# Two-unit lag for attention's transposes and values, later convolution products, and conditioning vectors from fp32r parts

## The chip, the cores and the metric

The kernel runs on one core of one Trainium2 chip. The metric is the device time of one execution in microseconds (us), as a median over runs. A difference of about 0.2% (6 us) is the least that a measurement of this kernel tells from no change.

The engines: PE (TensorE, matrix products), DVE (VectorE), ACT (ScalarE), POOL (GpSimd) and SP (which issues DMAs). Each engine takes its instructions in the order in which the program writes them; semaphores hold one engine back for another.

## The reference

Two layers of an encoder trunk are applied to a prompt of 512 tokens and to a sample of 256 tokens, width 1024. Cut to what matters here:

```python
for l in range(DEPTH):                                    # DEPTH = 2
    mod = (silu(c) @ ada_w[l] + ada_b[l]).reshape(B, 9, D)     # conditioning vectors
    h = x * (1 + mod[:, 1]) + mod[:, 0]
    x = layer_norm(ALPHA * x + 0.5 * (1 + mod[:, 2]) * swiglu_1(h))
    h = x * (1 + mod[:, 4]) + mod[:, 3]
    q, k, v, hz = split(h @ w_in[l])
    o_attn = window_attention(rope(q), rope(k), v, sink[l])    # |i - j| <= 128, softmax with a sink
    x0, x1, hv = split(short_conv(hz))
    filt = hyena_filters(L, ...)       # FFN with three sines, times a decay window
    o_hy = bidir_long_conv(hv * x1, filt) * x0                 # spectra: U * K, then inverse
    o = concat(rms_norm(o_attn), rms_norm(o_hy)) @ w_out[l]
    x = layer_norm(ALPHA * x + (1 + mod[:, 5]) * o)
    ...                                                        # second SwiGLU, layer norm
```

The diff touches three places of it: the first two conditioning vectors of layer 0, the long convolution, and the attention.

## The kernel before

**Numbers.** A product of two fp32 matrices is made of fp32r parts: ACT copies a tile to fp32r (the high part, `acopy`), DVE subtracts it from the original (the low part, `tt`), and PE runs three fp32r products, high by high, high by low, low by high. A plain fp32 product needs no parts, and shows as two records per product in the trace.

**Order.** The schedule is written by hand: every engine runs its instructions in program order. Tiles live in slots (`slot_s` 10, `slot_w` 6, `slot_r` 7, `slot_t` 6, `tiny` 12, and the 8 PSUM banks), and an allocation takes the free slot whose last use is oldest. All instructions come from one recording helper, so the profile shows them all at line 70; they are told apart by their tiles.

**The prologue** (from line 940). The filter FFN has three layers of `mlp` (two fp32 products on PE) and `sine` (seven DVE instructions and one ACT sine). Between them stand the calls of `ada_mm`: for i in 0 to 15, two fp32 products on 512 columns of `cc` (the silu of c) with a 512 KB tile of `ada_w`. The order is: sine 0, `ada_mm` 0 and 1, sine 1, `ada_mm` 2 to 4, sine 2, the decay rows of the filter, `ada_mm` 5 to 7, then six rounds of `tokens(t)` with `ada_mm(8 + t)`, a flush, `ada_mm` 14 and 15, and the spectra of the filters. `tokens(t)` is two fp32 products of 64 rows on PE, two multiplications by the window on DVE, the next window on ACT, and the split of the round before (two ACT copies, one subtraction on DVE, one on POOL). In rounds 0 and 4 DVE also adds a bias, in rounds 4 and 5 a sum and a difference.

**The mixer** (`run` in `mixer`, once per layer). Projection units 4 to 11 (48 products each) feed the convolution. `Hyena.products(a)` is DVE work: 16 tensor_tensor instructions on 512 columns for a = 0 and 1, 8 for a = 2, with ACT copies between; `inverse(a)` is 24 products on PE, `gate(a)` one DVE multiplication out of a bank. There are two Hyena halves, `hy0` and `hy1`, each with a = 0, 1, 2. `unit(i)` also calls `w_ahead(2)`, which splits the next weights (ACT copy, DVE subtraction). Then come three groups g of projections in three token pairs tp for keys and values and for the two halves of the queries: PE products, an ACT copy, rope on DVE, a split, and one step later the transposes of the result on PE (`transposed`). After each of these nine steps `side(i)` puts in other work.

**Attention** (`attention`, `Attention`). There are 12 units u of four heads each; units 4 to 7 of the key blocks in the middle have 384 keys (u = 6 to 9), the others 256. For one unit: `scores` (8 products on PE, then on DVE a masked copy with its maximum for each head, and small terms), `exps` (4 exponentials on ACT), `norms` (DVE sum and reciprocal, then the scaling of four heads), `turned` (8 or 12 transposes on PE and an ACT copy to high parts), `turned_lo` (DVE low parts), `values` (6 or 9 products on PE, ACT copy to `oT`). Round u of the loop runs `scores(u)`, `turned(u-1)`, `exps(u)`, `turned_lo(u-1)`, `filler`, `norms(u)`, `values(u-1)`. A `filler` is 12 products of the output projection on 512 and 256 columns; every second one ends in two DVE additions. `block_squares` (ACT square, two DVE additions) and the RMS steps stand between. DVE's own order in a round is thus: the maxima of `scores(u)`, `turned_lo`, `block_squares`, RMS steps, `norms(u)`, additions, and then the maxima of `scores(u+1)`.

Of the kernel before, what the change touches and what calls it, by code (L numbers as in the profile page):

```python
# [17 lines left out]
P = 128  # L18
D = 1024
# [141 lines left out]
def _program(mem, nc, x_in, c_col, c_row, w_units, ada_nat, ada_t, ada_b, ln_p, conv_p, sink_in, grp_in,  # L161
# [26 lines left out]
    def f32(ap):  # L188
        return ap.bitcast(F32)
# [764 lines left out]
    sp.dma_start(cc, c_col)  # L954
    act.activation(out=cc, in_=cc, func=AF.Silu)
    pa = [bank() for _ in range(4)]
    ada_raw = [slot_q([D]) for _ in range(4)]
# [8 lines left out]
    def ada_mm(i):  # L966
        raw = ada_raw[i]
        k, half = i // 2, i % 2
        for q in range(2):
            mm(pa[2 * half + q][:2, :512], cc[:, k, :], raw[:, q * 512:(q + 1) * 512], k == 0, k == ND - 1)  # L970
        if i + 4 < 16:
            ada_raw.append(slot_q([D]))
            sp.dma_start(ada_raw[i + 4], ada_nat[i + 4])
# [161 lines left out]
    def mods_part(i):  # L1135
        if i < 4:
            ams.append(slot_t([512]))
            acopy(ams[i][:2], pa[i][:2, :512])
        i -= 1
        am = ams[i] if i >= 0 else None  # L1140
        for j in range(4 if i >= 0 else 0):
            n = 4 * i + j
            pe.transpose(bt[:, 2 * n:2 * n + 2], am[:2, j * P:(j + 1) * P], idf[:2, :2])

# [4 lines left out]
    def skip():  # L1149
# [6 lines left out]
    gp.dma_start(ab, ada_b[:, 0, :2 * ND])  # L1156
    tt(mods[0][:, 0:2].rearrange("p m d s -> p (m d) s"), bt[:, :32].rearrange("p (n s) -> p n s", s=2),
       ab.unsqueeze(2).to_broadcast([P, 2 * ND, 2]), ALU.add)
    G, B = modul(0, 0, None)
# [27 lines left out]
    def mixer(l, x_prev, hh, hl):  # L1187
# [183 lines left out]
        def run(end):  # L1371
# [12 lines left out]
            u_transposes(1)  # L1384
            hy0.products(2)
            proj.unit(9)
            hy0.gate(0)
            hy0.inverse(1, dinv)
            hy1 = Hyena(1, u_spectrum(1, dfw))
            hy0.gate(1)  # L1390
            hy0.inverse(2, dinv)
            hy1.products(0)
            proj.unit(10)
            hy0.gate(2)
            hy1.products(1)
            proj.unit(11)
            hy1.inverse(0, dinv)
            hy1.products(2)
            hy1.gate(0)

# [4 lines left out]
            def side(i):  # L1405
                if i == 0:
                    hy1.inverse(1, dinv)
                    hy1.gate(1)
                elif i == 1:
                    hy1.inverse(2, dinv)  # L1410
                    hy1.gate(2)
                    rms[0].squares()
                elif i == 2:
                    rms[1].squares()
# [98 lines left out]
        class Attention:  # L1513
# [48 lines left out]
            def norms(self, u):  # L1562
                k0, k1 = self.keys(u)
                n = (k1 - k0) * P
                pv, sm = self.p[u], self.tinies.pop(u)
                es, den, rd = (sm[:, 4 * i:4 * i + 4] for i in range(3, 6))
                tt(den, den, es, ALU.add)
                vec.reciprocal(rd, den)
                for h in range(4):
                    if h < 2:  # L1570
                        ts(pv[:, h, :n], pv[:, h, :n], rd[:, h:h + 1], None)
                    else:
                        act.activation(out=pv[:, h, :n], in_=pv[:, h, :n], func=AF.Copy, scale=rd[:, h:h + 1])

# [30 lines left out]
        def attention(at, rms, on_hy, last_q, end):  # L1605
# [26 lines left out]
            fill = [(d, ks) for d in range(6) for ks in ((0, 1), (2, 3))]  # L1632
            share = (0, 0, 1, 1, 1, 1, 1, 1, 1, 1, 1, 2)
            fbank = {}
# [16 lines left out]
            rms_at = [Rms(oT, 0, s) for s in range(2)]  # L1651
            for u in range(1, 13):
                if 1 < u < 12:
                    at.scores(u)
                if u > 1:
                    at.turned(u - 1)
                    if u < 12:
                        at.exps(u)
                else:
                    filler()  # L1660
                    last_q()
                if u > 1:
                    at.turned_lo(u - 1)
                if done:
                    block_squares(done.pop())
                if u == 1:
                    rms[0].apply(on_hy, (2, 3))
                elif u == 2:
                    rms[1].apply(on_hy, (2, 3))
                    reload()  # L1670
                elif u == 6:
                    rms_at[1].Q = Q[0][:, SEQ[1]]
                    rms_at[1].stats()
                elif u == 7:
                    rms_at[1].bcast()
                    on_at.append(slot_s([2, 2, T], F32R))
                elif u == 8:
                    rms_at[1].apply(on_at, (0, 1))
                elif u == 11:
                    on_at.append(slot_s([2, 2, T], F32R))  # L1680
                    rms_at[1].apply(on_at, (2, 3))
                adds = [filler() for _ in range(share[u - 1])]
                if u < 12:
                    at.norms(u)
                for add in adds:
                    add()
                at.values(u - 1, oT)
                if at.units[u - 1][1]:
                    done.append(at.units[u - 1][0])
            block_squares(done.pop())  # L1690
# [235 lines left out]
```

## Time and profile before

| what | value |
|---|---|
| time, median of 3 runs | 2938.31 us (2937.6 to 2939.61) |
| time of the profiled execution | 2938.19 us |
| its span, first to last instruction | 2936.2 us |
| PE busy | 2837.5 us (97%) |
| DVE busy | 2139.2 us (73%) |
| ACT busy | 1367.5 us (47%) |
| POOL busy | 331.8 us (11%) |
| mean granted TensorE clock | 0.987 of full speed |

The profiled execution lasted 2.0 us more than its span and lies 0.1 us from the median of the runs, so a change of the span can be added to the median. The stages: prologue 0 to about 126 us, mixers about 690 to 1010 and 2090 to 2410 us, SwiGLU parts elsewhere. A view of waits lists who waited for whom, with the total, the number of times and the longest; a timeline lists instructions of one engine in order of time, equal neighbours merged (x12 means twelve), with the idle time before and its releaser in brackets. A merged line's time runs from the first start to the last end.

### The profile page before, as it was taken

The numbers are of one execution on the slowest core, as the hardware profiler recorded it, in microseconds if no ns is written. First come the engines' busy times: TensorE is split into PE (matmuls) and PEld (weight loads), VectorE is DVE, ScalarE is ACT, GpSimd is POOL, SyncE is SP. The second block draws the span as 40 slices with busy tenths as digits, with TensorE's granted clock in tenths as the row PEclk, the third lists the DMA queues.
The fourth block names the chain that finished last, engine by engine and source line by source line (L and its number), as shares of the span: only waits on it lengthen the run. The fifth ranks groups of instructions, "written<-read, shape, count | busy, mean of one in ns | idle before, by whom it ended". The sixth has DMA issues, their size and how long they took to land. (4 is left out here: it accounts for less than half of the span.)

```text
span 2936.2 us, 42164 instructions
## 1 busy us (share of the span) xinstructions
PE 2837.5 (97%) x16468; PEld 2594.4 (88%) x16468; DVE 2139.2 (73%) x3821; ACT 1367.5 (47%) x2355; POOL 331.8 (11%) x394
## 2 busy tenths in 40 slices
PE   9999999999998999999999999999999899999998
PEld 3789999988887889999988999998888788999997
DVE  5788778878967887777588777557896787444558
ACT  3544444444366544444445444444436644444444
POOL 2400000031000300000030000002100030000000
PEclk9999999999999999999999999999999999999999
DMA  5546665542121135664333665344212112455332
GB/s 202 194 171 173 188 176 164 147 151 103 57 73 51 65 127 161 194 194 116 107 122 122 179 176 157 107 107 145 102 63 73 51 57 89 85 115 115 97 108 83
DMA packets 102607, 364.65 MB, mean 124 GB/s; under 512 B 13750, under 2 KB 17031, under 8 KB 99208
## 3 DMA queue, kind: packets, MB, share of 16 engines
q1 hardware_dynamic: 74968, 259.88, 24.5%
q0 software_dynamic: 27440, 102.08, 16.2%
q8 instruction: 129, 2.11, 0.3%
q14 instruction: 70, 0.57, 0.1%
HBM read 284.33 MB, written 80.74 MB: 124 GB/s over the span
## 5 line engine op out<-in xcount | busy, mean ns | idle before, releaser
L70 PE MATMUL bank<-slot_s,slot_w 128*128 128x384 f32 (+2 forms) x13176 | 2322.1, 336 | 44.0 <-DVE slot_s L70 26.7
L70 PEld LDWEIGHTS bank<-slot_s,slot_w 128*128 128x128 f32 x13176 | 2130.5, 190 | 212.2 <-DVE slot_s L70 23.0
L70 DVE TENSOR_TENSOR slot_w<-slot_w,slot_w 128x1024 fp32r<-128x1024 f32 (+2 forms) x444 | 370.0, 864 | 4.1 <-ACT slot_w L70 1.6
L70 DVE CUSTOM_DVE_ANT_0 slot_t<-slot_r,slot_r 128x1024 bf16<-128x1024 f32 x256 | 311.4, 1223 | 77.4 <-DMA x_spill<-slot_t 45.0
L70 ACT ACTIVATE slot_w<-slot_w 128x1024 fp32r<-128x1024 f32 (+1 forms) x298 | 249.7, 838 | 119.2 <-DVE slot_w L70 118.9
L70 DVE TENSOR_TENSOR slot_w<-slot_r,slot_w 128x1024 fp32r<-128x1024 f32 (+1 forms) x194 | 222.0, 1153 | 113.4 <-ACT slot_w L70 111.9
L70 ACT ACTIVATE slot_t<-bank,tiny 128x512 f32<-128x512 f32 (+1 forms) x256 | 147.5, 580 | 307.9 <-PE bank L70 302.1
L70 POOL DMA_DIRECT2D x_spill<-slot_t x128 | 110.4, 862 | 1409.2 <-ACT slot_t L70 1409.2
L70 ACT ACTIVATE slot_w<-slot_r 128x1024 fp32r<-128x1024 f32 (+1 forms) x194 | 189.0, 992 | 155.9 <-DVE slot_r L70 98.1
L70 ACT ACTIVATE slot_t<-slot_t 128x384 f32<-128x384 f32 (+2 forms) x161 | 84.1, 526 | 334.2 <-DVE slot_t L70 334.0
L70 DVE TENSOR_TENSOR slot_t<-bank,slot_t 128x384 f32<-128x384 f32 x228 | 125.5, 555 | 144.2 <-PE bank L70 73.5
L70 DVE TENSOR_TENSOR slot_s<-slot_t,slot_s 128x768 fp32r<-128x768 f32 (+2 forms) x190 | 153.1, 810 | 52.6 <-ACT slot_s L70 48.4
L70 ACT ACTIVATE slot_s<-slot_t 128x768 fp32r<-128x768 f32 (+2 forms) x160 | 113.8, 717 | 159.9 <-DVE slot_t L70 155.5
L70 ACT ACTIVATE slot_t<-bank 128x384 f32<-128x384 f32 (+3 forms) x282 | 139.6, 495 | 101.6 <-PE bank L70 99.1
L70 PE MATMUL bank<-slot_s,slot_r 128*128 128x384 f32 x912 | 172.0, 337 | 0.0
L70 PEld LDWEIGHTS bank<-slot_s,slot_r 128*128 128x128 f32 x912 | 160.6, 188 | 0.0
L70 DVE TENSOR_TENSOR slot_r<-slot_w,slot_r 128x512 fp32r<-128x512 f32 x76 | 52.0, 684 | 106.4 <-ACT slot_r L70 106.4
L70 ACT ACTIVATE slot_t<-slot_s 128x256 f32<-128x256 f32 (+1 forms) x132 | 65.9, 510 | 108.0 <-DVE slot_s L70 104.1
L70 PE MATMUL bank<-slot_w,slot_s 128*128 128x256 f32 x864 | 107.9, 284 | 3.1 <-DVE slot_w L70 1.8
L70 PEld LDWEIGHTS bank<-slot_w,slot_s 128*128 128x128 f32 x864 | 104.7, 191 | 3.9 <-DVE slot_w L70 2.1
L70 DVE SCALAR_TENSOR_TENSOR slot_t<-bank,slot_t 128x384 f32<-128x384 f32 x76 | 42.3, 556 | 83.4 <-PE bank L70 82.2
L70 DVE SCALAR_TENSOR_TENSOR slot_s<-bank,tiny,slot_s 128x256 f32<-128x256 f32 (+1 forms) x160 | 87.0, 564 | 15.1 <-PE bank L70 14.9
(137 smaller groups left out, 2132.2 us busy)
## 6 DMA issues: line engine op xcount, KB each, us to landing
slot_r<-w_units SPq DMA_DIRECT2D x170, 512.0 KB, 4.8
slot_w<-w_units SPq DMA_DIRECT2D x146, 512.0 KB, 4.1
slot_r<-ada_t SPq DMA_DIRECT2D x128, 512.0 KB, 5.8
x_spill<-slot_t POOLq DMA_DIRECT2D x128, 384.0 KB, 5.3
slot_s<-x_spill POOLq DMA_DIRECT2D x12, 1536.0 KB, 8.2
x_spill<-slot_s POOLq DMA_DIRECT2D x10, 1024.0 KB, 4.6
slot_r<-ada_nat SPq DMA_DIRECT2D x16, 512.0 KB, 5.9
g_main<-slot_s POOLq DMA_DIRECT2D x4, 1536.0 KB, 10.0
```

The lines of the kernel that those rows point to most:

```text
L70: return getattr(real, name)(*args, **kwargs)
```

## The change

In the prologue `cc` is split into two parts in a tile of four columns (`cs`), and `ada_mm` splits each 512 KB tile (ACT copy, DVE subtraction) and multiplies both parts: four fp32r products instead of two fp32 products. The four rows of the result are transposed and added in pairs. In the mixer `hy0.products(2)` moves from behind the transposes of `hy1` to behind `hy0.gate(1)`; `hy1.products(0)` and `hy0.inverse(2)` move by one unit, and the three inverses of `hy1`, with `hy1.products(2)`, move into `side(0)` to `side(2)`. In the attention `turned` and `values` of a unit come two rounds behind its scores instead of one, with a thirteenth round at the end; fillers go one to a round from the second to the twelfth; RMS steps move by one round; in `norms` three heads are scaled on DVE and the fourth on POOL, where two were on DVE and two on ACT.

```diff
+    cs = const("cs", [ND, 4], F32R)
+    acopy(cs[:, :, 0:2], cc)
+    tt(cs[:, :, 2:4], cc, f32(cs[:, :, 0:2]), ALU.subtract)
...
         k, half = i // 2, i % 2
+        w = slot_w([2, D])
+        acopy(w[:, 0], raw)
+        tt(w[:, 1], raw, f32(w[:, 0]), ALU.subtract)
         for q in range(2):
-            mm(pa[2 * half + q][:2, :512], cc[:, k, :], raw[:, q * 512:(q + 1) * 512], k == 0, k == ND - 1)
+            for part in range(2):
+                mm(pa[2 * half + q][:4, :512], cs[:, k, :], w[:, part, q * 512:(q + 1) * 512],
+                   k == 0 and part == 0, k == ND - 1 and part == 1)
...
             u_transposes(1)
-            hy0.products(2)
             proj.unit(9)
             hy0.gate(0)
             hy0.inverse(1, dinv)
             hy1 = Hyena(1, u_spectrum(1, dfw))
             hy0.gate(1)
+            hy0.products(2)
+            proj.unit(10)
+            hy1.products(0)
+            proj.unit(11)
             hy0.inverse(2, dinv)
-            hy1.products(0)
-            proj.unit(10)
             hy0.gate(2)
             hy1.products(1)
-            proj.unit(11)
-            hy1.inverse(0, dinv)
-            hy1.products(2)
-            hy1.gate(0)
...
                 if i == 0:
+                    hy1.inverse(0, dinv)
+                    hy1.gate(0)
+                elif i == 1:
                     hy1.inverse(1, dinv)
+                    hy1.products(2)
                     hy1.gate(1)
-                elif i == 1:
+                    rms[0].squares()
+                elif i == 2:
                     hy1.inverse(2, dinv)
                     hy1.gate(2)
-                    rms[0].squares()
-                elif i == 2:
                     rms[1].squares()
...
                 for h in range(4):
-                    if h < 2:
-                        ts(pv[:, h, :n], pv[:, h, :n], rd[:, h:h + 1], None)
-                    else:
-                        act.activation(out=pv[:, h, :n], in_=pv[:, h, :n], func=AF.Copy, scale=rd[:, h:h + 1])
+                    ts(pv[:, h, :n], pv[:, h, :n], rd[:, h:h + 1], None, eng=gp if h == 3 else vec)
...
-            share = (0, 0, 1, 1, 1, 1, 1, 1, 1, 1, 1, 2)
+            share = (0,) + (1,) * 12
...
-            for u in range(1, 13):
+            o_hy.ahead = 1
+            for u in range(1, 14):
                 if 1 < u < 12:
                     at.scores(u)
-                if u > 1:
-                    at.turned(u - 1)
-                    if u < 12:
-                        at.exps(u)
-                else:
+                if u > 2:
+                    at.turned(u - 2)
+                if 1 < u < 12:
+                    at.exps(u)
+                if u == 1:
                     filler()
                     last_q()
-                if u > 1:
-                    at.turned_lo(u - 1)
+                if u > 2:
+                    at.turned_lo(u - 2)
...
-                at.values(u - 1, oT)
-                if at.units[u - 1][1]:
-                    done.append(at.units[u - 1][0])
+                if u > 1:
+                    at.values(u - 2, oT)
+                    if at.units[u - 2][1]:
+                        done.append(at.units[u - 2][0])
```

## Rows read from the trace of the kernel before

**Rows 1.** The page: the span, and busy time of each engine with its share.

```profile
span 2936.2 us, 42164 instructions
PE 2837.5 (97%) x16468; PEld 2594.4 (88%) x16468; DVE 2139.2 (73%) x3821; ACT 1367.5 (47%) x2355; POOL 331.8 (11%) x394
```

**Rows 2.** What PE waited for, whole span: total us, times, longest.

```profile
PE bank L70 <- DVE slot_w L70: 30.0, 26, 3.2
PE bank L70 <- DVE slot_s L70: 27.6, 18, 4.3
```

**Rows 3.** Timeline of PE in the prologue: start, us, instruction, idle before and releaser.

```profile
3.23 2.89 PE L70 MATMUL bank<-slot_t,slot_t 33*128 33x512 f32 x4 [3.23 <-DMA slot_t<-f_w]
...
13.37 1.56 PE L70 MATMUL bank<-slot_t,slot_t 128*128 128x512 f32 x4
14.86 5.31 PE L70 MATMUL bank<-slot_r,cc 128*2 128x512 f32 x12
...
27.95 1.98 PE L70 MATMUL bank<-slot_r,slot_t 64*128 64x512 f32 x4 [0.48 <-ACT slot_t L70]
...
53.70 3.06 PE L70 MATMUL bank<-slot_s,slot_w 128*128 128x512 f32 x12
```

**Rows 4.** Timeline of DVE in the prologue: last step of sine 1, a filter split.

```profile
19.01 0.64 DVE L70 TENSOR_SCALAR slot_t<-slot_t 128x768 f32<-128x768 f32 x1
...
38.08 0.68 DVE L70 TENSOR_TENSOR slot_s<-slot_t,slot_s 128x512 fp32r<-128x512 f32 x1
```

**Rows 5.** Timeline of ACT in the prologue: sine 0.

```profile
10.51 0.84 ACT L70 ACTIVATE slot_t<-slot_t 128x768 f32<-128x768 f32 x1 [5.65 <-DVE slot_t L70]
```

**Rows 6.** The page's costliest groups: splitting a 1024-column tile, busy, mean ns.

```profile
L70 DVE TENSOR_TENSOR slot_w<-slot_r,slot_w 128x1024 fp32r<-128x1024 f32 (+1 forms) x194 | 222.0, 1153 | 113.4 <-ACT slot_w L70 111.9
L70 ACT ACTIVATE slot_w<-slot_r 128x1024 fp32r<-128x1024 f32 (+1 forms) x194 | 189.0, 992 | 155.9 <-DVE slot_r L70 98.1
```

**Rows 7.** Timeline of PE: twelve fp32r products on 512 columns.

```profile
106.65 2.95 PE L70 MATMUL bank<-slot_r,slot_w 128*128 128x512 f32 x12
```

**Rows 8.** Timeline of PE in the convolution of layer 0.

```profile
759.43 2.53 PE L70 MATMUL bank<-slot_s,slot_w 128*128 128x256 f32 x12 [4.34 <-DVE slot_s L70]
...
781.99 3.04 PE L70 MATMUL bank<-slot_w,slot_w 128*128 128x256 f32 x24
...
788.49 4.46 PE L70 MATMUL bank<-slot_w,slot_s 128*128 128x256 f32 x35 [0.88 <-DVE slot_w L70]
...
801.42 0.81 PE L70 MATMUL bank<-ident,slot_r 128*128 128x128 f32 x8
```

**Rows 9.** Timeline of DVE there: first of 16 products, last rope split.

```profile
761.30 0.68 DVE L70 TENSOR_TENSOR slot_r<-slot_s,slot_s 128x512 f32<-128x512 f32 x1
...
798.60 0.42 DVE L70 TENSOR_TENSOR slot_t<-slot_t,slot_t 128x256 fp32r<-128x256 f32 x1
```

**Rows 10.** Window 760 to 765 us: busy PE, PEld, DVE, ACT, POOL, granted clock, DMA.

```profile
760.00:765.00 5.00, 5.00 (x32) 5.00 (x31) 4.93 (x9) 1.19 (x2) 0.00 (x0) 0.67 0.08 34
```

**Rows 11.** What DVE waited for, 855 to 945 us: the longest of five, all on ACT.

```profile
DVE slot_t L70 <- ACT slot_t L70: 8.6, 5, 2.1
```

**Rows 12.** Timeline of DVE, units 8 and 9: first maximum, scaling, next first maximum.

```profile
909.89 0.55 DVE L70 CUSTOM_DVE_ANT_0 slot_w<-bank,mask 128x384 f32<-128x384 f32 x1
...
916.40 0.75 DVE L70 TENSOR_SCALAR slot_w<-slot_w,tiny 128x384 f32<-128x384 f32 x2
917.06 0.55 DVE L70 CUSTOM_DVE_ANT_0 slot_w<-bank,mask 128x384 f32<-128x384 f32 x1
```

**Rows 13.** Timeline of PE: transposes of the last attention unit of layer 0.

```profile
941.40 2.02 PE L70 MATMUL bank<-ident,slot_w 128*128 128x128 f32 x8 [3.20 <-DVE slot_w L70]
```

**Rows 14.** Groups of POOL by form: scaling 256 columns, count, busy, mean ns.

```profile
L70 POOL TENSOR_SCALAR slot_s<-slot_t,lnp 128x256 f32<-128x256 f32 x40 | 27.0, 675 | 25.2 <-DVE slot_t L70 23.2 <-ACT slot_r L70 0.9 <-ACT slot_s L70 0.5
```

**Rows 15.** Timeline of POOL late in the prologue: one subtraction.

```profile
115.27 1.34 POOL L70 TENSOR_TENSOR slot_s<-slot_t,slot_s 128x512 fp32r<-128x512 f32 x1 [0.43 <-DVE slot_t L70]
```

**Rows 16.** Timeline of DVE at the same time: one scaling of 512 columns.

```profile
115.38 1.51 DVE L70 TENSOR_SCALAR slot_t<-slot_s,tiny,tiny 128x512 f32<-128x512 f32 x1
```

More of the change, by code (lines that the diff above doesn't have):

```diff
@@ L1137, in mods_part @@
             ams.append(slot_t([512]))
-            acopy(ams[i][:2], pa[i][:2, :512])
+            acopy(ams[i][:4], pa[i][:4, :512])
         i -= 1
@@ L1142, in mods_part @@
             n = 4 * i + j
-            pe.transpose(bt[:, 2 * n:2 * n + 2], am[:2, j * P:(j + 1) * P], idf[:2, :2])
+            pe.transpose(bt[:, 4 * n:4 * n + 4], am[:4, j * P:(j + 1) * P], idf[:4, :4])
     def sides(*fs):
@@ L1156, in _program @@
     gp.dma_start(ab, ada_b[:, 0, :2 * ND])
-    tt(mods[0][:, 0:2].rearrange("p m d s -> p (m d) s"), bt[:, :32].rearrange("p (n s) -> p n s", s=2),
-       ab.unsqueeze(2).to_broadcast([P, 2 * ND, 2]), ALU.add)
+    first_mods = mods[0][:, 0:2].rearrange("p m d s -> p (m d) s")
+    for i in range(2):
+        tt(first_mods, bt[:, :64].rearrange("p (n s) -> p n s", s=4)[:, :, 2 * i:2 * i + 2],
+           first_mods if i else ab.unsqueeze(2).to_broadcast([P, 2 * ND, 2]), ALU.add)
     G, B = modul(0, 0, None)
@@ L1670, in attention @@
                     reload()
-                elif u == 6:
+                elif u == 7:
                     rms_at[1].Q = Q[0][:, SEQ[1]]
                     rms_at[1].stats()
-                elif u == 7:
+                elif u == 8:
                     rms_at[1].bcast()
                     on_at.append(slot_s([2, 2, T], F32R))
-                elif u == 8:
+                elif u == 9:
                     rms_at[1].apply(on_at, (0, 1))
-                elif u == 11:
+                elif u == 12:
                     on_at.append(slot_s([2, 2, T], F32R))
                     rms_at[1].apply(on_at, (2, 3))
-                adds = [filler() for _ in range(share[u - 1])]
+                adds = [filler() for _ in range(share[u - 1]) if fill]
                 if u < 12:
```

## The prediction

> **What bounds the kernel now.** I read the page first: PE is busy 97% of a span of 2936.2 us [rows 1], so outside a few stretches only less work on PE, or fewer of its waits, can make this kernel faster. Then the view of PE's waits: of the time PE stood still, 30.0 us went to DVE results in `slot_w` and 27.6 us to DVE results in `slot_s` [rows 2]. These are the waits that the two reorderings are near. Third, the timelines of PE, DVE and ACT side by side in the three stretches that the diff touches. That is where the question is settled, because a wait of PE disappears only if the engine that it waits for is not itself the bound.
>
> **Prologue, what goes.** The timeline of PE runs with hardly a gap from 3.2 us to the first spectra at 53.70 us. Six fp32 products took 5.31 us, 0.885 us each [rows 3], so the 32 of `ada_mm` take 28.3 us. Twelve fp32r products on 512 columns took 2.95 us [rows 7], 0.246 us each, so the 64 new ones take 15.7 us. PE is relieved of 12.6 us. Were PE still the bound, that would be the gain.
>
> **Prologue, what comes.** Sixteen ACT copies of 0.99 us and sixteen DVE subtractions of 1.15 us [rows 6], 15.9 and 18.4 us. What covers them? In the kernel before, `ada_mm` needed only its tile and `cc`, so PE ran it while DVE and ACT computed the sines. Now its second product waits for DVE, and DVE takes its instructions in order: the subtraction for `ada_mm(0)` stands behind sine 0, and the copy for it on ACT stands behind the ACT sine. PE also takes its instructions in order, so `mlp` of the next sine waits behind `ada_mm`. The work that hid the sines becomes a link of the same chain. I add it up along that chain.
>
> Sine 0 leaves ACT at 11.35 us [rows 5]. A copy (1.0), two subtractions (2.3) and the last products end at about 15.6 us, where `mlp` 1 began at 13.37 [rows 3]: 2.2 us late. From the end of `mlp` 1 (14.93) to the end of sine 1 on DVE (19.65) are 4.7 us [rows 3, 4], and an ACT sine takes 0.84 [rows 5]. Then copy, three subtractions, three products: 1.0 + 3.45 + 0.15 + 0.7 = 5.3 us; `mlp` 1.56 [rows 3]; 4.7; the sine 0.84; again 5.3 us for `ada_mm` 5 to 7. From 15.6 that is 15.6 + 1.56 + 4.7 + 0.84 + 5.3 + 1.56 + 4.7 + 0.84 + 5.3 = 40.4 us. The decay rows, a DVE instruction on 1024 columns (1.2 us by the nearest row [rows 6]), stand ahead of the last three subtractions and overlap the sine and the first copy, and each handover costs 0.1 to 0.2 us: some 42 us. The rounds of `tokens` began at 27.95 [rows 3], so they begin 14 to 15 us late.
>
> A round took 3.7 us, bound by PE. Now: two products 1.98 [rows 3], 0.2 to DVE, the second window product and the split of the round before at 0.68 each (same shape as the row of the split [rows 4]), the subtraction 1.15, 0.15 back to PE, three fp32r products 0.7: 5.5 us. Rounds 4 and 5 have five more DVE instructions of 0.68 between them, 3.4 us, and `ada_mm` 14 and 15 with the last split add 3.0: 6 x 5.5 + 3.4 + 3.0 = 39.4 us, against 25.7 us from 27.95 to 53.70 [rows 3]. With the 14 us this makes the spectra begin about 28 us late with PE at full clock.
>
> PE's clock is the open price here. The first `mlp` took 2.89 us for four records where the second took 1.56 [rows 3], and after a wait of 4.34 us the mean granted clock of the next 5 us was 0.67 [rows 8, 10], a mix of 1.2 and 2.4 GHz. In the new prologue PE stands still for some 5 us during each of the last two sines and for about 2.5 us in each round. At the lower level an `mlp` costs 1.3 us more and a round some 2.3 us more (1.98 and 0.7 nearly double). Ends: no loss, 28 us; lower level throughout, 28 + 3 + 6 x 2.3 + 2 = 47 us. I take the lower level in the sines and the first one or two rounds, nearest to the row where the mean of 0.67 means 3.3 us of 5 at the lower level [rows 10]: **33 us slower**. From the spectra on PE was gapless and the rest of the prologue only shifts. The SP queue issues the later `ada_w` tiles when subtractions free their slots, several rounds ahead of use, and `x` behind them still lands before its use.
>
> **Convolution, in each of two layers.** PE waited 4.34 us for a bank that DVE had to read (its convolution steps stood behind `hy0.products(2)`) and 0.88 us, with about as much once more just before, for weights that stood behind `products(1)` [rows 8]; after the first wait 12 products took 2.53 us, 1.0 more than half of the 24 in 3.04 [rows 8], and the next ones some 0.6 more. Together 7.6 us. The move takes `hy0.products(2)` out of the way, so these go, except some 0.7 us for the second weight tile of the keys, still behind 16 products. What is late next: `hy1.products(1)`, 16 x 0.68 = 10.9 us [rows 9], now stands after `unit(11)` and ahead of the first rope. PE came to its first rope transposes at 801.42 [rows 8]; without the waits, and with one inverse of 3.04 us [rows 8] moved behind them, it would be there at about 791. DVE finished that rope at 799.0 [rows 9]; it saves the 8 x 0.68 = 5.4 us of `hy1.products(2)`, so about 794. PE waits some 3 us there, new, perhaps with 1 us of slow clock. Gain 7.6 - 0.7 - 3 - 1 = **2.9 us** a layer; ends 0 and 7.
>
> **Attention, in each of two layers.** The change takes PE off the wait for `norms`. But DVE, in its order, does the maxima of unit u, waits for the exponentials, scales, and only then takes the maxima of unit u + 1; this order stays. From 855 to 945 us DVE waited only for ACT, never for PE [rows 11], and one turn for 384 keys took 7.17 us [rows 12] without additions. So a PE that is ahead stands still elsewhere, and the end of the last `norms` hardly moves. On this ring: a third scaling on DVE, half of 0.75 us for 384 keys [rows 12], about 0.3 on average over 11 units, +3.3 us; two ACT scalings fewer ahead of the exponentials, at most 3 us back, as these seldom started late; the squares and RMS step of the last round now behind the ring, 2 us back; a shorter tail after the transposes at 941.40 [rows 13], where the products of one filler no longer follow, about 1 us back. Together 2.7 us gained.
>
> The fourth head on POOL takes about 0.7 us (0.675 for 256 columns [rows 14]), and its reader comes a round later. But a DVE scaling that began 0.1 us after a POOL instruction ended 0.28 us after it and took 1.51 us, four times the 0.375 us of a scaling of 384 columns [rows 12, 15, 16]. Unknown is whether POOL gets in between DVE's scalings: from 0 to 0.65 us a unit, 0 to 7 us a layer; I take half, 3.3 us. So attention comes to about **0** (+0.6), ends -6 and +4 us. The Trainium skill ("SBUF — State Buffer", section "Who interferes with whom") states an exclusive lock on a port pair, where the second to issue blocks fully; the two rows agree. By it alone the price would be the full 7 us a layer whenever POOL comes between.
>
> **Sum.** 33 - 2 x 2.9 + 2 x 0.6 = +28 us. The profiled execution (2938.19 us) lies 0.1 us from the median, so 2938.3 + 28 = **2966 us**.
>
> **The rivals.** (1) PE's waits in the mixers go altogether: 30.0 + 27.6 us [rows 2] less those outside, plus slow clock, some 26 us a layer; 33 - 52 gives 2919 us. The place is the attention ring; it decides faster from the point where a layer gives back over 20 us. For it: PE did name DVE as releaser there. Against it: DVE's waits are on ACT, and that ring is kept. Half of it gives 2945. (2) The splits are hidden: ACT and DVE do them in idle time and PE's 12.6 us come off, 2938 - 13 - 5 = 2920 us. For it, DVE idles up to 4 us before each sine; against it, that idle time lies behind the sine in the queue. (3) The low clock holds through the rounds and POOL comes between the scalings: 47 + 8 - 2, about 2990 us. For it, PE would be busy only about half the time; against it, no wait in a round is as long as 4.34 us. (4) The reorderings do not do what they say (a slot's reuse brings the old wait back): 2938 + 33 + 2 = 2973, inside my case.
>
> **How the numbers follow.** Forecast with (4), 2952 to 2980: 0.62. (3): 0.15. (1): whole 0.06, half 0.09. (2): 0.08. The range from 2938 to 2988 us leaves out the whole of (1) and (2) and the end of (3), under 0.2. An amount of 0.2% is 6 us, about what a measurement here can tell from no change: faster 0.14, the same 0.09, slower 0.77.
>
> **What would show it.** Right: the first spectra at 82 to 95 us instead of 53.70; PE waiting on `slot_w` from DVE in the prologue; in the attention still DVE on ACT and hardly a shorter turn; a new PE wait on `slot_r` ahead of the first rope transposes. Wrong: spectra before 55 us, or turns of the ring below 6.5 us at 384 keys.

## The result and the profile after

The changed kernel took 2987.8 us, median of 4 runs (2985.2 to 2992.7), against 2939.0 us of the kernel before (2937.6 to 2943.0): a ratio of 1.0166, 95% interval 1.0148 to 1.0183, or 48.8 us more. The forecast was 2966 us, 28 us more, with a range to 2988: the sign was right, the size was short by 21 us. The result lies inside the range by 0.2 us only, and that is luck: the attention came out beyond the upper end that the text gave it.

The page after, to be read beside [rows 1]: the span is 48.6 us longer, and PE is busy only 8 us longer; for the other 40 us it stood idle. At full clock its new products would be 12.6 us less work, so some 20 us of slow clock (8 + 12.6, an estimate) stand inside the busy time. The mean granted clock fell from 0.987 to 0.976.

```profile
span 2984.8 us, 42251 instructions
PE 2845.5 (95%) x16468; PEld 2602.4 (87%) x16468; DVE 2175.1 (73%) x3863; ACT 1363.7 (46%) x2324; POOL 360.1 (12%) x418
```

What PE waited for, whole span, to be read beside [rows 2] (total us, times, longest). The two groups on DVE hardly moved in sum (57.6 us before, 53.1 now), but they moved in place: of the 26.4 us on `slot_w`, 18.4 lie in the first 100 us, where the kernel before had none up to its first spectra. The group on ACT's `slot_w` holds three waits of over 6 us:

```profile
PE bank L70 <- DVE slot_s L70: 26.7, 22, 2.4
PE bank L70 <- DVE slot_w L70: 26.4, 25, 3.4
PE bank L70 <- ACT slot_w L70: 23.7, 5, 6.6
PE bank L70 <- ACT slot_s L70: 14.8, 8, 5.1
```

**Prologue.** The timeline of PE (start, us, instruction, idle before and its releaser), to be read beside [rows 3]:

```profile
25.39 0.59 PE L70 MATMUL bank<-slot_w,cs 128*4 128x512 f32 x1 [6.34 <-ACT slot_w L70]
...
43.60 1.98 PE L70 MATMUL bank<-slot_r,slot_t 64*128 64x512 f32 x4
...
48.81 3.15 PE L70 MATMUL bank<-slot_r,slot_t 64*128 64x512 f32 x4
...
71.76 3.78 PE L70 MATMUL bank<-slot_r,slot_t 64*128 64x512 f32 x4
75.47 0.59 PE L70 MATMUL bank<-slot_w,cs 128*4 128x512 f32 x1
79.45 1.44 PE L70 MATMUL bank<-slot_w,cs 128*4 128x512 f32 x3 [3.40 <-DVE slot_w L70]
80.83 3.78 PE L70 MATMUL bank<-slot_r,slot_t 64*128 64x512 f32 x4
...
94.29 4.30 PE L70 MATMUL bank<-slot_s,slot_w 128*128 128x512 f32 x12
```

The rounds begin at 43.60 us (27.95 before) and the first spectra at 94.29 (53.70 before), 40.6 us late. The two products of `tokens` take 1.98 us in the first round, as before, 3.15 in the second and 3.78 in each of the last four. The windows say why (us, busy time and count of PE, PEld, DVE, ACT, POOL, then the granted clock, DMA): the clock is 0.50, its lower level of 1.2 GHz, in all nine windows of 5 us from 50 to 95 us, and each of the rows below has a PE that is idle for part of the time or has just been.

```profile
50.00:55.00 5.00, 3.00 (x6) 0.63 (x5) 3.12 (x4) 2.28 (x5) 0.48 (x1) 0.50 0.12 50
80.00:85.00 5.00, 5.00 (x8) 1.25 (x5) 0.98 (x2) 0.00 (x0) 0.54 (x1) 0.50 0.01 3
85.00:90.00 5.00, 1.60 (x5) 0.34 (x4) 4.96 (x6) 3.16 (x4) 1.93 (x2) 0.50 0.00 0
```

**Convolution.** In layer 0 the stretch from the transposes of `u` (739.51 us before, 779.80 after) to the scores of unit 0 (840.09 before, 877.23 after) went from 100.6 to 97.4 us. The long wait of [rows 8] is gone. The one for weights stays, and a new one stands ahead of the first rope transposes, followed by products at low clock (24 in 4.51 us, 3.04 in [rows 8]):

```profile
818.91 4.45 PE L70 MATMUL bank<-slot_w,slot_s 128*128 128x256 f32 x35 [0.88 <-DVE slot_w L70]
...
833.66 1.28 PE L70 MATMUL bank<-ident,slot_r 128*128 128x128 f32 x8 [1.65 <-ACT slot_r L70]
834.74 4.51 PE L70 MATMUL bank<-slot_w,slot_w 128*128 128x256 f32 x24
```

**Attention.** From the scores of unit 0 to the first transposes of the row statistics behind the attention (`ident,tiny`), it took 122.9 us before and 130.1 after. The wait of PE on DVE's `slot_w`, which the lag was to end, is almost gone from this stretch (first line before, second after), but all of PE's waits in it rose from 17 to 22 us:

```profile
PE bank L70 <- DVE slot_w L70: 12.0, 8, 3.2
```

```profile
PE bank L70 <- DVE slot_w L70: 0.6, 2, 0.5
```

The timeline of PE has two waits in it that the kernel before did not have, at 907 and at 992 us:

```profile
877.23 1.21 PE L70 MATMUL bank<-slot_s,slot_s 128*128 128x256 f32 x8 [1.00 <-ACT slot_s L70]
...
907.22 1.89 PE L70 MATMUL bank<-slot_s,slot_w 128*128 128x256 f32 x6 [5.08 <-ACT slot_s L70]
...
992.29 0.80 PE L70 MATMUL bank<-slot_s,slot_w 128*128 128x256 f32 x2 [2.29 <-ACT slot_w L70]
...
1007.32 0.60 PE L70 MATMUL bank<-ident,tiny 128*128 128x128 f32 x4
```

And on DVE the scaling of `norms` got longer. Two heads of 384 columns took 0.75 us [rows 12]; three now take 1.74 us with POOL's scaling of the fourth beside them, and 1.41 us in one unit. POOL's row begins 0.16 us after DVE's first in both cases; what makes the one unit shorter is not shown. Timeline of DVE, the first maximum of unit 6, the scalings of units 6 and 7, and the first maximum of unit 10:

```profile
933.77 0.54 DVE L70 CUSTOM_DVE_ANT_0 slot_w<-bank,mask 128x384 f32<-128x384 f32 x1
...
940.41 1.74 DVE L70 TENSOR_SCALAR slot_w<-slot_w,tiny 128x384 f32<-128x384 f32 x3
...
948.65 1.41 DVE L70 TENSOR_SCALAR slot_w<-slot_w,tiny 128x384 f32<-128x384 f32 x3
...
969.31 0.41 DVE L70 CUSTOM_DVE_ANT_0 slot_w<-bank,mask 128x256 f32<-128x256 f32 x1
```

The same two maxima in the kernel before:

```profile
892.86 0.55 DVE L70 CUSTOM_DVE_ANT_0 slot_w<-bank,mask 128x384 f32<-128x384 f32 x1
...
926.33 0.41 DVE L70 CUSTOM_DVE_ANT_0 slot_w<-bank,mask 128x256 f32<-128x256 f32 x1
```

The four turns with 384 keys took 33.5 us before and 35.5 after, each time with the additions of two fillers.

POOL's scalings of the fourth head in units 6 and 7 after the change:

```profile
940.57 1.37 POOL L70 TENSOR_SCALAR slot_w<-slot_w,tiny 128x384 f32<-128x384 f32 x1 [6.87 <-PE bank L70]
...
948.81 1.60 POOL L70 TENSOR_SCALAR slot_w<-slot_w,tiny 128x384 f32<-128x384 f32 x1 [0.70 <-PE bank L70]
```

DVE's waits in the attention, 893 to 985 us, to be read beside [rows 11]: still on ACT, as forecast, and now once on PE, behind the wait at 907 us.

```profile
DVE slot_t L70 <- ACT slot_t L70: 5.8, 4, 1.9
DVE tiny L70 <- ACT tiny L70: 3.6, 4, 1.2
DVE slot_s L70 <- ACT slot_s L70: 2.4, 3, 1.7
DVE slot_w L70 <- PE bank L70: 1.9, 1, 1.9
```

**The account of the trace**: prologue about +40, convolution about -3 in each layer, attention +7 in each layer: 40 - 6 + 14 = 48 us.

### The profile page after: what moved, and what is told of

Same layout as the page of the kernel before. It is cut to its first block, busy times and chain, and to the rows that moved or that the text cites. A ratio compares the mean times of both kernels' runs of the same rounds, so it can differ in the third digit from the quotient of the medians.

```text
span 2984.8 us, 42251 instructions
## 1 busy us (share of the span) xinstructions
PE 2845.5 (95%) x16468; PEld 2602.4 (87%) x16468; DVE 2175.1 (73%) x3863; ACT 1363.7 (46%) x2324; POOL 360.1 (12%) x418
## 5 line engine op out<-in xcount | busy, mean ns | idle before, releaser
L70 DVE TENSOR_TENSOR slot_w<-slot_r,slot_w 128x1024 fp32r<-128x1024 f32 (+1 forms) x210 | 241.0, 1157 | 112.0 <-ACT slot_w L70 110.5
L70 ACT ACTIVATE slot_w<-slot_r 128x1024 fp32r<-128x1024 f32 (+1 forms) x210 | 205.2, 996 | 150.6 <-DVE slot_r L70 94.1
```

What stands on the lines that cost most here:

```text
L70: return getattr(real, name)(*args, **kwargs)
```

## The experiments

The theory after reading the trace: (a) the prologue's loss is PE waiting for splits it just asked for, and the low clock that follows; (b) the attention's loss is POOL's port, the filler in round 2 and the shorter look ahead for weights, while the ring of maxima, exponentials and scalings stays what it was. The rivals stand with each experiment. All times are medians; "us" of a ratio is what it lies above 1, times 2938. A trace shows one execution: those of e5 and e1 took 4 and 3 us more than their medians, those of e6, e9 and e7 5, 4 and 4 us less, so a price read from one trace is good to some microseconds.

### Which part costs what: e1_prologue, e2_mixers, e3_conv

e1 is the kernel before with the change's prologue; e2 with the moves in convolution and attention, the prologue as before; e3 with those of the convolution alone. Their diffs are the corresponding parts of the diff above.

> The kernel before with the change's first part alone: the conditioning products as fp32r parts, with their copies and subtractions; mixers untouched. My theory after the change's trace (its first spectra began at 94.3 us instead of 53.7): this part alone costs about 40 us, so some 2979 us (2975 to 2984), first spectra at 93 to 96 us. Rival A, the forecast of 33 us or less, with the rest lost in the mixers: 2966 to 2972 us. Rival B, the parts interact (the mixers lose more because the prologue ends late): under 2966 us.

> The kernel before with the two reorderings of the mixers alone (convolution and attention); prologue untouched. My theory from the shifts in the changed kernel's trace (-3.2 and -2.9 us in the two convolutions, +7.2 us in each of the two attentions): +8 us, 2946 us (2943 to 2950). The forecast for these parts: -5 us, 2934 us. Rival: the waits of the tensor engine in the mixers go after all, and only the late prologue hides it: below 2925 us.

> The kernel before with the moves in the convolution alone: products(2) of the first convolution and inverse(0), products(2) of the second put later; attention's units and prologue untouched. My theory: -3 us in each of two layers, 2933 us (2930 to 2935), a new wait of 1 to 3 us of the tensor engine ahead of the first rope transposes. Rival: the moved products only push the same vector work into the attention's first rounds, and what is gained is given back there: 2937 to 2941 us.

| kernel | median us | ratio to before | 95% interval | us |
|---|---|---|---|---|
| e1_prologue | 2980.2 | 1.0149 | 1.0135 to 1.0162 | +44 |
| e2_mixers | 2942.0 | 1.0017 | 1.0008 to 1.0026 | +5.0 |
| e3_conv | 2931.1 | 0.9981 | 0.9973 to 0.9990 | -5.6 |

e1 and e3 came inside the theory's ranges, e2 1 us below its own (2943 to 2950). The parts add up: 44 + 5 = 49 us, what the whole change cost. The moves in the convolution are a gain, and it isn't given back: e3's attention, taken as above, is 122.8 us long in layer 0 (834.54 to 957.36 us) as before, and 124.4 against 123.1 us in layer 1. So the attention's edits cost 5.0 + 5.6 = 10.6 us by the medians, and the prologue nine tenths of the whole.

### The prologue: load, wait or clock: e5_load, e6_warm, e9_lag3, e12_lagwarm

e5 keeps the fp32 products and adds the copies and subtractions, into a slot that nothing reads:

```diff
         raw = ada_raw[i]
         k, half = i // 2, i % 2
+        w = slot_w([2, D])
+        acopy(w[:, 0], raw)
+        tt(w[:, 1], raw, f32(w[:, 0]), ALU.subtract)
         for q in range(2):
             mm(pa[2 * half + q][:2, :512], cc[:, k, :], raw[:, q * 512:(q + 1) * 512], k == 0, k == ND - 1)
```

> The kernel before with the new load and without the new dependency: each ada_w tile is copied by the scalar engine and subtracted by the vector engine as in the change, into a slot that nothing reads, and the fp32 products stay as they were, on the raw tile. Theory: what costs is that the products wait for the split and that the tensor engine then runs at the lower clock, not the work on the other engines: 2937 to 2946 us, rounds longer only where the vector engine's own 16 subtractions of 1.15 us exceed its room. Rival: the load itself is the price, since the sines and window products stand behind it on the vector engine: 2960 us or more, first spectra after 76 us.

It took 2945.8 us, ratio 1.0024 (1.0015 to 1.0033), +7 us, at the upper end of the theory's range. Its trace shows of what the loss is made:

```profile
31.11 3.78 PE L70 MATMUL bank<-slot_r,slot_t 64*128 64x512 f32 x4 [3.58 <-ACT slot_t L70]
34.81 3.57 PE L70 MATMUL bank<-slot_r,cc 128*2 128x512 f32 x4
...
48.08 1.88 PE L70 MATMUL bank<-slot_r,cc 128*2 128x512 f32 x4
...
64.48 3.06 PE L70 MATMUL bank<-slot_s,slot_w 128*128 128x512 f32 x12
```

The rounds begin 3.2 us late, because sine 2 now stands behind subtractions. PE had waited 3.58 us, and then ran the first two rounds without a gap but at the lower level (3.78 and 3.57 us for what takes 1.98 and 1.88). From 31.11 to 64.48 us are 33.4 us, 7.6 more than in [rows 3]. The load itself is a small part of 44 us, and a wait of a few microseconds on PE was followed by a loss twice its length.

e6 is the change's prologue with products that nothing reads, in the gaps of PE:

```diff
+    def warm(n):
+        for _ in range(n):
+            mm(dummy[:4, :512], cs[:, 0, :], last_w[0][:, 0, :512], True, True)
...
+        if i > 7:
+            warm(9)
...
-    sine(hid, mlp(w23[:, 0, :], hid, P), 1)
+    ps = mlp(w23[:, 0, :], hid, P)
+    warm(24)
+    sine(hid, ps, 1)
```

(the same behind `mlp` 2).

> The change's prologue alone, plus products whose result nothing reads, to fill the tensor engine's waits: 24 after each of mlp 1 and mlp 2, 9 in each ada_mm from 8 on (of 512 columns, fp32r). Theory: the rounds took 7.7 us or more because the products ran at the lower clock for all of 50 to 95 us; held at the higher level a round takes 5.5 to 6.5 us and the first spectra begin at 80 to 87 us, 2964 to 2973 us in all. Rival: a round is bound by the copies and subtractions, whatever the clock: first spectra at 93 us or later and 2978 us or more.

It took 2972.6 us, ratio 1.0112 (1.0095 to 1.0128), +33 us: by the ratios 11 less than e1, although PE has more to do. The clock was 1.00 in every window of 5 us from 20 to 105 us. Its timeline of PE, with the starts of the first and the last two rounds and of the spectra, to be read beside 43.60, 71.76, 80.83 and 94.29 above:

```profile
41.81 1.98 PE L70 MATMUL bank<-slot_r,slot_t 64*128 64x512 f32 x4
...
63.44 1.98 PE L70 MATMUL bank<-slot_r,slot_t 64*128 64x512 f32 x4
...
70.50 1.98 PE L70 MATMUL bank<-slot_r,slot_t 64*128 64x512 f32 x4
...
83.12 2.92 PE L70 MATMUL bank<-slot_s,slot_w 128*128 128x512 f32 x12
```

The last full round takes 7.1 us, where it took 9.1. So holding the clock up gave back 11 of the 40 us to the first spectra; the waits are the other 29. The 11 is net of the time that the unread products take themselves, and it is rough: in e1's trace, with the same prologue as the change, the first spectra began at 97.0 us and not at 94.3.

e9 keeps the fp32r products and gives them distance: two calls of `ada_mm` stand between a tile's split and its products, and the parts stand in `slot_s`.

```diff
+    held = []
     def ada_mm(i):
         raw = ada_raw[i]
-        w = slot_w([2, D])
+        w = slot_s([2, D], F32R)
         acopy(w[:, 0], raw)
         tt(w[:, 1], raw, f32(w[:, 0]), ALU.subtract)
+        held.append((i, w))
-        for q in range(2):
...
+        if i > 2:
+            ada_out()
...
+    def ada_out():
+        i, w = held.pop(0)
+        k, half = i // 2, i % 2
+        for q in range(2):
...
```

> The change's prologue alone, but the products of an ada_w tile come two calls of ada_mm after its split (the parts stand in slot_s, so that three can be held); copies, subtractions and products are the same in number. Theory: the 43 us come from the products waiting for the split just issued, and from the low clock that follows; with two calls in between the tensor engine waits only where it did with the mere load, first spectra at 52 to 64 us, 2936 to 2948 us in all. Rival: the vector engine's order alone makes the rounds long, whichever product waits: first spectra at 85 us or later, 2970 us or more.

It took 2951.9 us, ratio 1.0046 (1.0032 to 1.0059), +13.5 us: between the two ranges, much nearer the theory's; the first spectra came at 69.77 us, where the theory had 52 to 64. The distance takes back 30 of the 44 us. (No run parts it from the change of slots; but the waits in the change's prologue name the copy and the subtraction, not a slot.) What is left is seen in rows of its PE timeline and in one window:

```profile
31.09 2.56 PE L70 MATMUL bank<-slot_r,slot_t 64*128 64x512 f32 x4 [3.74 <-ACT slot_t L70]
...
51.90 3.78 PE L70 MATMUL bank<-slot_r,slot_t 64*128 64x512 f32 x4
...
69.77 2.92 PE L70 MATMUL bank<-slot_s,slot_w 128*128 128x512 f32 x12
```

```profile
50.00:55.00 5.00, 5.00 (x9) 1.50 (x8) 3.38 (x5) 3.15 (x4) 1.27 (x1) 0.50 0.05 21
```

PE is busy for 5.00 of 5 us and yet at 0.50: a round takes 5.5 us with no gap in it. The last experiment asks whether that clock is all that is left. It adds unread products to e9: two in `ada_out`, seven behind `mlp` 0, fourteen behind `ada_mm` 2 to 4 and again behind 5 to 7:

```diff
+        if 5 < i < 13:
+            warm(2)
...
+    for _ in range(7):
+        mm(dummy[:, :512], w1[:33, :], zt[:33, :512], True, True)
...
+    warm(14)
```

> The prologue with the lag of two calls, plus products whose result nothing reads: 7 behind mlp 0, 14 behind the products that follow mlp 1 and mlp 2, 2 with each tile from 6 to 12. With the lag alone PE had no gap from 35 to 66 us and yet stood at half its clock there, 69.8 us to the first spectra, 2951.9 us in all. Theory: that clock is all that is left of the loss; held at the higher level a round takes 3.4 to 4 us instead of 5.5, first spectra at 54 to 60 us, 2936 to 2943 us. Rival: the vector engine's queue sets the rounds, at any clock: first spectra at 66 us or later, 2948 us or more.

It took 2953.3 us, ratio 1.0060 (1.0040 to 1.0081), no better than e9. The experiment is not clean: the seven products behind `mlp` 0 held PE longer than the wait they were to fill, and the rounds began at 36.55 instead of 31.09 us. But the rounds themselves can be read. At the higher level they take 3.4 us, and DVE has hardly a gap then. The timeline of PE, then two windows (DVE is the third busy time):

```profile
53.48 1.98 PE L70 MATMUL bank<-slot_r,slot_t 64*128 64x512 f32 x4
...
56.86 1.98 PE L70 MATMUL bank<-slot_r,slot_t 64*128 64x512 f32 x4
...
71.38 3.93 PE L70 MATMUL bank<-slot_s,slot_w 128*128 128x512 f32 x12
```

```profile
50.00:55.00 5.00, 5.00 (x15) 1.76 (x14) 5.00 (x7) 4.76 (x7) 1.82 (x2) 1.00 0.64 210
55.00:60.00 5.00, 5.00 (x18) 1.60 (x17) 4.93 (x7) 2.20 (x4) 1.30 (x1) 1.00 0.00 0
```

The rounds to first spectra take 34.8 us, against 38.7 in e9 and 25.8 before. This speaks for the rival: 9 us above the kernel before are left, and three of PE's waits in this stretch are on DVE (1.93, 2.27 and 1.75 us). It does not prove it, as the clock was not up throughout (0.79 and 0.87 from 40 to 50 us, 0.68 and 0.64 from 65 to 75). The 12.6 us that PE saves show up in the time of no run.

### The attention: e4_lag_act, e10_three, e7_share, e8_ring, e11_ahead

Each goes on from e2, the prologue as before. e4 has the old scalings back (two heads on DVE, two on ACT); e10 has three on DVE and the fourth on ACT, so that only POOL's scaling is taken out and given to ACT (the diff is that of e10; e4 has `h < 2`):

```diff
                 for h in range(4):
-                    ts(pv[:, h, :n], pv[:, h, :n], rd[:, h:h + 1], None, eng=gp if h == 3 else vec)
+                    if h < 3:
+                        ts(pv[:, h, :n], pv[:, h, :n], rd[:, h:h + 1], None)
+                    else:
+                        act.activation(out=pv[:, h, :n], in_=pv[:, h, :n], func=AF.Copy, scale=rd[:, h:h + 1])
```

> As the two reorderings together, but the scalings as in the kernel before: two heads on the vector engine, two on the scalar engine, none on GpSimd. Theory: the third scaling on the vector engine and its wait for the port that GpSimd holds cost 8 us in eleven units of a layer, of which 3 us were won on the scalar engine; without them each attention is 3 to 8 us shorter, 2932 to 2940 us. Rival: the scalings lie off the ring and the loss is the wait of the filler in round 2 for the RMS step of the same round: 2944 to 2948 us, as with all of it.

> The two reorderings with three scalings on the vector engine and the fourth on the scalar engine, none on GpSimd: it parts the price of the third scaling from that of the port. With the old scalings it was 2934 us, with the change's 2942. Theory: most of the 8 us is the port that GpSimd holds: 2934 to 2937 us. Rival: the third scaling in the ring (0.3 us in each of 22 units) is the price: 2940 to 2943 us.

e7 is e4 without a filler in round 2:

```diff
-            share = (0,) + (1,) * 12
+            share = (0, 0) + (1,) * 11
```

> As the two reorderings with the old scalings, but no filler in round 2: its products begin in round 3, and one more comes in round 13. Theory: the wait of 4 to 5 us in round 2, for the part that the RMS step of the same round makes, goes, and half or more of it arrives at the end of the attention: 2 to 5 us less a layer than with the filler there, 2924 to 2930 us. Rival: the ring of maxima, exponentials and scalings catches up within the later rounds anyway: 2933 to 2936 us.

e8 is e7 with `norms` of a unit put one round later, and the block's squares ahead of the exponentials, so that DVE takes the maxima of unit u before it needs any exponential of that unit, and then scales unit u - 1, whose exponentials are a round old:

```diff
                 if u > 2:
                     at.turned(u - 2)
+                if done:
+                    block_squares(done.pop())
                 if 1 < u < 12:
                     at.exps(u)
+                if 1 < u < 13:
+                    at.norms(u - 1)
...
-                if u < 12:
-                    at.norms(u)
```

> As the one without a filler in round 2, with norms of unit u - 1 put behind the maxima and exponentials of unit u, and the block's squares ahead of the exponentials: the vector engine no longer has to wait for a unit's exponentials before it takes the next unit's maxima. Theory: what sets the attention's length is that ring, which the change kept; with the ring opened, turns shorten by about 1 us and each attention by 6 to 12 us: 2905 to 2920 us. Rival: the tensor engine or the scalar engine is the next bound at once: 2924 to 2932 us, as without the edit.

e11 is e8 without the line `o_hy.ahead = 1`, so with the old look ahead of two tiles.

> The opened ring, without the line that sets o_hy.ahead to 1, so that the fillers split their weights two tiles ahead as before the change. Theory: the wait of 2.3 us on slot_w at the end of each attention comes from that line; without it 2 to 5 us less than the opened ring's 2921: 2916 to 2919 us. Rival: the splits ahead only move scalar work into the ring, which gets longer by as much: 2921 to 2926 us.

The attention stretch is taken in each trace from the scores of unit 0 to the `ident,tiny` transposes, as above; for the kernel before these are 840.09 to 962.94 us in layer 0 and 2235.64 to 2358.70 us in layer 1. This is better than absolute times, since the unchanged code ahead of the mixers differs by up to 4 us between profiles (the transposes of `u` came at 739.51 us before and at 735.56 in e2).

| kernel | layer 0 us | layer 1 us | median us | ratio to before (95%) |
|---|---|---|---|---|
| before | 122.9 | 123.1 | 2937 to 2939 | |
| e3: convolution alone | 122.8 | 124.4 | 2931.1 | 0.9981 (0.9973 to 0.9990) |
| e2: all of it | 130.0 | 129.6 | 2942.0 | 1.0017 (1.0008 to 1.0026) |
| e10: no POOL | 125.7 | 124.3 | 2933.8 | 0.9987 (0.9979 to 0.9996) |
| e4: old scalings | 123.9 | 123.6 | 2934.3 | 0.9989 (0.9980 to 0.9999) |
| e7: no filler in round 2 | 123.2 | 120.4 | 2929.9 | 0.9972 (0.9962 to 0.9983) |
| e8: ring opened | 119.5 | 119.4 | 2921.1 | 0.9940 (0.9926 to 0.9954) |
| e11: two tiles ahead | 117.4 | 117.5 | 2918.1 | 0.9931 (0.9917 to 0.9944) |

**POOL** is the largest single price: 4.8 us a layer by the traces, 8 us in two layers by the medians. The third scaling on DVE, less what ACT saves, costs little beside it: 1.3 us a layer by the traces, nothing by the medians. DVE's scalings of layer 0 together bear this out: 8.0 us in e4, 11.4 in e10 and 17.0 in e2. One line of the same unit (unit 6) from e10 and one from e2 show it: three scalings take 1.08 us without POOL and 1.75 us with POOL beside them.

```profile
894.21 1.08 DVE L70 TENSOR_SCALAR slot_w<-slot_w,tiny 128x384 f32<-128x384 f32 x3
```

```profile
896.02 1.75 DVE L70 TENSOR_SCALAR slot_w<-slot_w,tiny 128x384 f32<-128x384 f32 x3
```

The Trainium skill ("SBUF — State Buffer", section "Who interferes with whom") says of DVE in its two-port modes that whichever of DVE and GpSimd issues first holds the shared ports for its whole instruction and the other blocks. Whether these scalings ran in such a mode no row tells. The rows agree that the two hold each other up, 0.67 us here. They don't show a block for a whole instruction: POOL's row beside them lasts 1.37 us, and DVE's loss falls on two scalings (0.74 us each instead of 0.41).

**The filler in round 2** costs 1.9 us a layer (0.7 in layer 0, 3.2 in layer 1; medians: 5 us in two), just under the 2 to 5 us that were expected: it needs heads that the RMS step of the same round makes. The old kernel had no filler there.

**The ring.** With `norms` a round later, and the squares moved in the same edit, each attention is 2.3 us shorter by the traces and the kernel 9 us faster by the ratios. The two don't agree: e7's runs spread from 2924.5 to 2935.7 us, and its trace is one of the fast ones. 2921 us lies just above the theory's range and below the rival's, so the ring was a bound, but less of one than expected. The order shows in the first maxima of units 2 and 11: 67.0 us apart before, 74.5 in the changed kernel, 65.1 in e7 and 62.4 in e8 (layer 0). Among DVE's waits from 830 to 1000 us, e7 has the one of `norms` for the sums of the exponentials:

```profile
DVE tiny L70 <- ACT tiny L70: 3.6, 4, 1.0
```

In e8 it is gone, and the maxima begin to wait for PE instead (0.2 us in e7):

```profile
DVE slot_w L70 <- PE bank L70: 3.4, 4, 1.4
```

**Look ahead**: 2.0 us a layer. The 3 us by the medians are alone less than a measurement here can tell, but with the line away PE's wait of 2.29 us on `slot_w` behind the last unit is gone, as expected.

e11 is faster than both kernels: 2918.1 us, 0.7% under the kernel before. It is the moves in the convolution and the lag of two units, without POOL, with `norms` a round later, two tiles of look ahead and no fp32r prologue.

## Why the prediction fell short

**Prologue, forecast +33, measured +40 (trace) to +44 (medians).** The chain was right: PE waits for each split, and the split stands behind the sine. The sums at full clock were 42 us for the start of the rounds and 28 us of delay for the spectra; e6, with the clock held, began the rounds at 41.81 us and the spectra 29.4 us late. So close a fit is in part luck, since the 0.1 to 0.2 us for each handover stand in no row. The term that was off is the clock. The text took the lower level "in the sines and the first one or two rounds", 5 us, by [rows 10], where it held for 3.3 of 5 us. It held from the second round to the first spectra, and cost 11 us (94.29 against 83.12 us in e6). The price per round was right: rounds 2 to 5 lost 1.8 to 2.4 us each, where the text had 2.3. Which rounds pay it was misjudged. The first did not, and the sines cost 1.8 us (43.60 against 41.81 us at the start of the rounds); with 0.8 us from the sixth round to the spectra that makes the 11. The upper end, 19 us, had all six rounds pay, and more in the sines.

The reason given against the low clock, in rival (3), was that no wait in a round is as long as 4.34 us. The waits in the rounds were 2.0 to 3.4 us, and the clock stayed at 0.50 all the same; in e9 it stayed there for five windows without any wait.

**Convolution, forecast -2.9 a layer, measured -2.8 (e3) and -3.2 (trace).** Right in kind: the long wait went, 0.88 us stayed at the weights, and a wait with slow clock came ahead of the first rope transposes. That wait was shorter than forecast, 1.65 us for 3, and the slow clock behind it dearer, 1.9 us for 1 (1.28 and 4.51 us against 0.81 and 3.04), so the two misses nearly cancel. Its releaser was ACT's `slot_r`, one step behind the rope on DVE.

**Attention, forecast +0.6 a layer, measured +5.3 (e2 less e3) to +7.0 (trace).** Here the step failed, beyond its own upper end of +4. Taken apart, by the traces of the experiments: POOL 4.8 us where 3.3 was taken, half of the 0 to 7 (a unit of 384 columns lost 0.67 us in the rows above, the end of the range, where the text took half); the third scaling, less what ACT saves, 1.3 where 0.3 was taken; and two waits that the text did not have, the filler in round 2 with 1.9 and the shorter look ahead with 2.0 (measured in the opened ring). These are 10.0; the stretch grew by 6.8 in e2, so some 3 us came back, as the forecast had for the squares and the shorter tail, though no run parts these two. The mis-sized terms make 2.5 us, the two missing ones 3.9. What was missed is that an edit of the order also moves what stands between: `share` put a filler into the round that makes its input, and `ahead` took splits from the tail. Both lines stood in the diff, and the text costed neither.

**What was said of the ring held.** DVE waited on ACT as before, the turns did not shorten (35.5 us for four, 33.5 before), and a PE that is ahead gained little by it: e7, with the lag but without POOL and the filler in round 2, took 2929.9 us, e3 without the lag 2931.1. e8 shows it from the other side: the lag pays once `norms` follows it.

**The rivals.** (1) and (2) are out: e2, with the prologue of before, is no faster than before, and e9, with a distance of two calls between split and product, is still 13.5 us behind. (4) is out as well, since the long waits that the reorderings aimed at did go. (3), at 2990 us, came within 2 us of the result, with the right mechanisms and the wrong split, so the nearness of its number is luck: 11 us of clock where it took 19, and 7 us a layer in the attention of which POOL is 5.

## What to carry to other kernels

Work that hid a chain's latency stops hiding it once it takes an input from the same engines: look in whose queue, and behind what, each new input stands, and give it a distance of a round or more before counting what PE saves. Even then the engine that makes the input can be the next bound: with distance, 13.5 us of the loss were left here. When a step is moved, walk through every line of the loop again for the inputs of that round (a filler, a look ahead), and not only along the wait that the move is meant to end. A reordering that took PE off a wait paid here only when the engine waited for was freed of its own ring; that was one more move, `norms` a round later, worth 9 us by the medians where the only part of the change that gained, the convolution, gave 5.6.

## What the hardware showed beyond that

- In e9 PE was busy for 5.00 of 5 us in five windows in a row, 35 to 60 us, and the granted clock stayed at 0.50 in all of them, behind a wait of 3.74 us. In e5 the same `tokens` products with fp32 products between them were back at full clock in the third round, after some 15 us without a gap. In the kernel before, where PE's longest wait between 13 and 54 us was 0.50 us, it was 1.00 from 15 us to the first spectra. What decides when the clock comes back, no run here settles: a busy PE in the rows is not enough. Unread products kept it up in e6 and brought it to 1.00 again in e12 (0.79 and 0.87 in the windows from 40 to 50 us, 1.00 from 50 to 65).
- Three DVE scalings of 384 columns took 1.08 us without POOL (e10) and 1.75 us with a POOL scaling begun during them (e2). The POOL scaling took 1.37 to 1.60 us itself, and 0.91 to 0.99 us for 256 columns, where 0.675 us is the mean of a scaling of that size elsewhere in the kernel before [rows 14].
